# A two-layer block on one core: the first four projection units side by side over quarters of K

## The chip, the core and the metric

The kernel runs on one NeuronCore of a Trainium2 chip. The core has a matrix engine (TensorE, PE in the profile), two elementwise engines (VectorE, DVE, and ScalarE, ACT), GpSimd (POOL) and SyncE (SP), which here only issues DMAs. Each engine works through its own instructions in order. The metric is the device time of one execution in microseconds, the median over several runs.

## What is computed

A first block (normalisation, one wide projection, three kinds of attention over 256 tokens, gated up-projection, output projection, residual) feeds a second one (modulation, two recurrent scans in both directions, a gated feed-forward layer with a convolution). All of it is float32. What matters here is the very first stage:

```python
def rmsnorm(x, g):                       # x: 1 x 256 x 2048
    y = x * lax.rsqrt(jnp.mean(x * x, axis=-1, keepdims=True) + EPS)
    return y * g
hn = rmsnorm(x, norm_g)
proj = jnp.einsum('bsd,dc->bsc', hn, w_in)   # K = d = 2048
br = proj[..., :QKVG_COLS].reshape(b, s, 3, 4, 512)
qa = rmsnorm(to_heads(br[:, :, 0, 0]), ...)  # branch 0: q, then k, v, gate
ka = rmsnorm(to_heads(br[:, :, 0, 1]), ...)
```

## The kernel before

**Precision.** Each float32 operand is split in two parts that TensorE takes at its faster float32 rate: a rounded high part (ScalarE, a copy) and the remainder (VectorE, original less rounded part). A product is then high x high, high x low and low x high. Activations lie as tiles of K, `h(k)` and `l(k)`, 128 x 256 each (K on partitions, tokens along the row), side by side in memory. Weights come in chunks `wr` of 128 x 1024 (eight K tiles of 128 columns), which `Lead.high` rounds into `wh` (ScalarE) and `Lead.low` subtracts into `wl` (VectorE).

**Units.** The projections are a list of units (`f_unit`, L325). A unit makes 128 output columns for all 256 tokens over K = 2048, that is 16 K tiles, as two halves of one chunk each. For every K tile there is one wide matmul (`wh` against `h(k)` and `l(k)` together, 512 columns) and one narrow one (`wl` against `h(k)`, 256 columns); in odd pieces of a unit the narrow ones go first. All accumulate in one accumulator `pm`, of which there are four. After its last half a unit's `post` joins the two column halves (one ScalarE and one VectorE instruction) and gives the accumulator back; in branch 0 the result is later multiplied by the row factor `r1`, since the first projection runs on x times gain, and the normalisation by the mean square is put in afterwards.

**Order.** `first_block` (L850) queues, for branch 0, four units of k, four of q, the forget rows, v and the gate. The program is one loop over `flat`, the list of (unit, half); every engine's order is the order in which this loop writes instructions. For entry i it issues the weight load of entry i + 7, rounds up to i + 4, subtracts up to i + 3, advances side tasks by one step (`W.step`), then issues the matmuls of entry i. There are five `wr` buffers, so the load of chunk e waits until chunk e - 5 has been rounded and subtracted; all weight loads are issued by SP, in order. There are five `wh` and four `wl` buffers.

**The opening.** `start` (L589) runs ahead of the loop. SP loads x's first quarter (`xs[0]`, in two pieces), weight chunk 0, `xs[1]`, chunk 1, `xs[2]` and `xs[3]`; ScalarE's queue loads the first 96 columns of a vector of small parameters (with the gain of the norm at `V_NG`), GpSimd the rest and an identity. Then, quarter by quarter, the 16 x tiles are multiplied by the gain, rounded (ScalarE) and subtracted (VectorE, L200), with chunks 0 and 1 in between. `stats`, a side task, squares the four quarters of x (ScalarE), sums them (three VectorE additions), and sums over partitions by matmuls against ones (`ssq_rstd`, accumulator `ps`), from which `r1` comes; it begins at the loop's second entry, and its matmuls stand in TensorE's order ahead of those of entry 6. `norm1` waits for `r1`, makes the normalised activations for the other branches and starts the modulation work, which streams a large weight through VectorE as filler. A helper records each operation, so many instructions share a line: L166 is every matmul, L184 every ScalarE copy, L191 every two-input VectorE operation.

Of the kernel before, what the change touches and what calls it, by code (L numbers as in the profile page):

```python
# [12 lines left out]
AF = mybir.ActivationFunctionType  # L13
ALU = mybir.AluOpType
# [5 lines left out]
KT = D // 128  # L20
# [109 lines left out]
def trunk_kernel(  # L130
# [50 lines left out]
    def act(out, in_, func, **kw):  # L181
        W.cost["act"] += width(out) / 1200.0 + 0.18
        load_table(func)
        nc.scalar.activation(out=out, in_=in_, func=func, **kw)  # L184
# [105 lines left out]
    def col(c, n=1):  # L290
        return vec[:, c:c + n]
# [30 lines left out]

    units, rush = [], set()

    def f_unit(src, acts, post, nk=KT, k0=0, first=True, last=True, box=None, cols=512, folded=False):  # L325

        box = box if box is not None else {}
        if folded:  # L330
            cols = 256

        def pre():
            box["a"] = acts()
            if first:
                W.take("pm")
                box["acc"] = pm((128, cols))

        def pe(i, h, l):
            acc, a = box["acc"], box["a"]  # L340
            n = min(8, nk - 8 * i)
            end = last and 8 * i + n == nk
            ks = [(k0 + 8 * i + j, slice(j * 128, j * 128 + 128)) for j in range(n)]
            if cols == 512:

                def wide():
                    for k, w in ks:
                        mm(acc, lhsT=h[:, w], rhs=a.both(k), start=k == 0, stop=end and k == k0 + nk - 1)

                def narrow():  # L350
                    for k, w in ks:
                        mm(acc[:, 0:256], lhsT=l[:, w], rhs=a.h(k), start=False, stop=False)

                for part in (narrow, wide) if i % 2 else (wide, narrow):
                    part()
                return
            for k, w in ks:
                stop = end and k == k0 + nk - 1
                if folded:
                    w = slice(w.start, w.start + 96)  # L360
                    if k:
                        mm(acc[0:96, :], lhsT=h[:, w], rhs=a.l(k), start=False, stop=False)
                    mm(acc, lhsT=h[:, w.start:w.start + 128], rhs=a.h(k), start=k == 0, stop=stop)
                    if k == 0:
                        mm(acc[0:96, :], lhsT=h[:, w], rhs=a.l(k), start=False, stop=False)
                else:
                    mm(acc, lhsT=h[:, w], rhs=a.h(k), start=k == 0, stop=False)
                    mm(acc[:, 0:256], lhsT=h[:, w], rhs=a.l(k), start=False, stop=False)
                    mm(acc, lhsT=l[:, w], rhs=a.h(k), start=False, stop=stop)

        halves = [(c * 128, min(8, nk - c) * 128) for c in range(0, nk, 8)]
        units.append(Unit(src, halves, pe, pre, (lambda: W.spawn(post(box["acc"]), urgent=True)) if last else None, folded))
        return box

# [214 lines left out]
    def start():  # L589
        W.room["s4"] -= 4 + 8 + 2  # L590
        xs = [slot() for _ in range(4)]
        u = Acts()
        nc.scalar.dma_start(out=vec[:, 0:V_QK], in_=vec_d[:, 0:V_QK])
        load_table(AF.Ln)
        for i in (0, 2):
            nc.sync.dma_start(out=xs[0][:, i:i + 2, :], in_=xT[:, i:i + 2, :])
        lead.load(0)
        nc.sync.dma_start(out=xs[1], in_=xT[:, 4:8, :])
        lead.load(1)
        nc.sync.dma_start(out=xs[2], in_=xT[:, 8:12, :])  # L600
        nc.sync.dma_start(out=xs[3], in_=xT[:, 12:16, :])
        nc.gpsimd.dma_start(out=vec[:, V_QK:NV], in_=vec_d[:, V_QK:NV])
        nc.gpsimd.dma_start(out=ident, in_=ident_d)
        nc.gpsimd.memset(ones, 1.0)
        nc.gpsimd.memset(epsc, EPS)
        nc.gpsimd.memset(hot, 0.0)
        nc.gpsimd.memset(hot[:, 7:8], 1.0)
        for j in range(4):
            u.more()
            for i in range(4):  # L610
                k = 4 * j + i
                g = col(V_NG + k)
                act(out=u.h(k), in_=xs[j][:, i, :], func=AF.Copy, scale=g)
                stt(out=u.l(k), in0=xs[j][:, i, :], scalar=g, in1=u.h(k), op0=ALU.mult, op1=ALU.subtract)
            if j < 2:
                lead.low(j)
        st["u"] = u

        def stats():
            yield from rest(1)  # L620
            tot = slot()
            for j in range(4):
                q = slot() if j else tot
                act(out=q, in_=xs[j], func=AF.Square)
                yield
                if j:
                    tt(out=tot, in0=tot, in1=q, op=ALU.add)
            yield
            r = yield from ssq_rstd([tot[:, j, :] for j in range(4)])
            give(s4=2)  # L630
            st["r1"] = r
            yield from rest(3)
            yield from grab(ps=1)
            p = ps((128, 2))
            for b in range(2):
                mm(p[:, b:b + 1], lhsT=r[0:1, b * 128:b * 128 + 128], rhs=ones[0:1, 0:1], start=True, stop=True)
            vcopy(rT, p)
            give(ps=1)
            st["rT"] = True

        def norm1():
            yield from until_has("r1")
            r = st["r1"]
            act(out=hot_r, in_=hot, func=AF.Copy)
            act(out=act_c, in_=col(V_C, 32), func=AF.Silu)
            W.idle = st["mod"] = W_mod()
            h = Acts()
            yield
            yield from normed(h, xs, r, col(V_NG, 16))
            st["h"] = h  # L650
            yield from grab(s4=1)
            t = cslot(K_LEV)
            yield from rest(4)
            act(out=lmask, in_=t[:, 0:896].rearrange("p (a b) -> p a b", b=128), func=AF.Copy)
            give(s4=1)

        W.spawn(stats(), urgent=True)
        W.spawn(norm1())
        tt(out=sel[0:36, :], in0=ident[0:36, 0:4], in1=ident[0:36, 32:36], op=ALU.add)
        gq = gqk  # L660
        for j in range(4):
            ts(out=gq[:, j:j + 1], in0=col(V_QK + j), scalar1=SCALE if j % 2 == 0 else 1.0, scalar2=None, op0=ALU.mult)

    gqk = cp.tile([128, 4], F32, name="gqk")
    rT = cp.tile([128, 2], F32, name="rT")
# [184 lines left out]
    def first_block():  # L850
        it = iter(range(10 ** 6))
        nxt = lambda: w1[next(it)]
        for n in range(NB):
            b = {}
            source = u1 if n == 0 else h1
            for key in "kq":
                for hh in range(NH):
                    def post(p, n=n, b=b, key=key, hh=hh):
# [9 lines left out]
                        if hh == NH - 1:  # L868
# [3 lines left out]
                                b["t" + key] = W.spawn(head_norm(x, gqk[:, j:j + 1]))  # L872
                            if key == "q":
                                W.spawn(attend(n, b))
                    f_unit(nxt(), source, post)
            if n == 0:
                f_unit(wf1, u1, forget_rows, folded=True)

# [1145 lines left out]
    ctx_units()  # L2024
    lat_block()
    ffn()
    flat = [(u, i) for u, x in enumerate(units) for i in range(len(x.halves))]

    class Lead:

# [36 lines left out]
    with tc.manual_schedule():  # L2067
        start()
        for i, (u, j) in enumerate(flat):
            lead.load(i + 7)  # L2070
            if u in rush:
                W.step()
# [165 lines left out]
```

## Time and profile before

| | us |
|---|---|
| median of 3 runs | 2126.79 |
| lowest and highest | 2124.09, 2127.64 |
| the profiled execution, by its own clock | 2121.56 |
| its span, first to last instruction | 2119.8 |

The profiled execution is one run of its own; the time outside its span is 1.8 us. In the rows further down, PE is TensorE's matmuls, PEld its weight loads (which overlap with the matmuls), and an engine's name with a q is its DMA issue or sequencer. A DMA's row gives the time of issue; the landing time is given by the views of a line or tile. "x8" behind a row of the order of time is the number of instructions merged in it, and the bracket tells how long the engine was idle before it and what released it. A matmul's duration includes its run through the array, so consecutive ones overlap; their spacing is shorter than their duration.

### The profile page before, as it was taken

To read this page: it belongs to the slowest core of one execution; us is meant where nothing else is said; L and a number is where in the kernel's file an instruction comes from. 1 tells how busy PE (TensorE), PEld (TensorE's weight loads), DVE (VectorE), ACT (ScalarE), POOL (GpSimd) and SP (SyncE) were. 2 spreads that over 40 slices of the span, in tenths; PEclk is the share of its full clock that TensorE was granted. 3 is DMA by queue.
4 is the path that set the end of the run, shared out by engine and by line. 5 is a ranking of instruction groups with operands and counts; after the bars stand their busy time and mean duration, and the time that the engine had idled before them with its cause. 6 is when DMAs were issued, how large, how long until landed. Compare 5 with 4: busy or idle time off the path is not lost.

```text
span 2119.8 us, 31753 instructions
## 1 busy us (share of the span) xinstructions
PE 2083.6 (98%) x11834; PEld 1814.0 (86%) x11834; DVE 1734.4 (82%) x2499; ACT 1134.5 (54%) x1653; POOL 125.5 (6%) x251
## 2 busy tenths in 40 slices
PE   8999999999999999999999999999999999999997
PEld 6888888998988887888888788888888888888886
DVE  6999897999999988778876757789888888897554
ACT  6765555454545656555645545555555555543542
POOL 0010100000111010110000000000000000021000
PEclk9999999999999999999999999999999999999999
DMA  7686776777799796885444445646555555598653
GB/s 276 230 284 215 260 246 210 257 241 275 271 329 396 251 338 222 312 326 200 162 161 158 149 148 202 223 141 204 194 189 189 189 190 189 187 384 318 197 188 115
DMA packets 140283, 488.52 MB, mean 230 GB/s; under 512 B 15424, under 2 KB 21584, under 8 KB 140128
## 3 DMA queue, kind: packets, MB, share of 16 engines
q1 hardware_dynamic: 105344, 366.13, 48.7%
q0 software_dynamic: 32784, 119.40, 16.2%
q8 instruction: 92, 1.51, 0.3%
q10 hardware_dynamic: 2000, 0.97, 0.2%
q14 instruction: 63, 0.52, 0.1%
HBM read 479.10 MB, written 7.34 MB: 229 GB/s over the span
## 4 chain that ended last, share of the span: by engine, by line
PE 94%; DVE 2%; DMA 1%; issue 1%; ACT 1%; POOL 0%; DVEq 0%; SPq 0%; ACTq 0%; POOLq 0%
PE pm L166 86%; PE ps L166 7%; DMA s<-in_wmod_dram 1%; DVE wl L191 1%; DVE a L200 1%; DVE s L191 1%; ACT wh L184 0%; ACT s L184 0%; DVE s L200 0%; DMA wr<-in_w_dram 0%; PE ps L170 0%; ACT b L184 0%; DVE a L191 0%; ACT L177 0%; DVE b L191 0%
## 5 line engine op out<-in xcount | busy, mean ns | idle before, releaser
L166 PE MATMUL pm<-s,wh 128*128 128x512 f32 (+3 forms) x5019 | 1163.5, 377 | 8.7 <-ACT wh L184 8.7
L184 ACT ACTIVATE wh<-wr 128x1024 fp32r<-128x1024 f32 x706 | 727.8, 1034 | 627.5 <-PE pm L166 488.8
L166 PEld LDWEIGHTS pm<-s,wh 128*128 128x128 f32 (+1 forms) x5019 | 898.0, 189 | 164.3 <-ACT wh L184 8.7
L191 DVE TENSOR_TENSOR wl<-wr,wh 128x1024 fp32r<-128x1024 f32 (+2 forms) x700 | 826.2, 1192 | 186.3 <-issue 82.6
L166 PE MATMUL pm<-s,wl 128*128 128x256 f32 (+1 forms) x4635 | 657.9, 283 | 9.2 <-DVE wl L191 7.4
L166 PEld LDWEIGHTS pm<-s,wl 128*128 128x128 f32 x4635 | 615.9, 191 | 35.0 <-DVE wl L191 9.0
L200 DVE SCALAR_TENSOR_TENSOR s<-s,act_c,s 128x1024 f32<-128x1024 f32 x240 | 301.8, 1278 | 14.3 <-DMA s<-in_wmod_dram 13.7
L166 PE MATMUL pm<-wh,s 128*128 128x512 f32 x832 | 262.6, 397 | 0.0
L166 PEld LDWEIGHTS pm<-wh,s 128*128 128x128 f32 x832 | 154.3, 188 | 35.4 <-issue 3.3
L166 PE MATMUL pm<-wl,s 128*128 128x512 f32 x416 | 162.3, 390 | 0.0
L200 DVE SCALAR_TENSOR_TENSOR a<-b,vec,a 128x192 f32<-128x192 f32 (+1 forms) x344 | 149.2, 434 | 9.1
L414 POOL DMA_DIRECT2D s<-in_wmod_dram x188 | 99.1, 528 | 931.1 <-DVE s L200 438.0
L191 DVE TENSOR_TENSOR s<-pm,s 128x256 f32<-128x256 f32 x142 | 59.7, 421 | 46.7 <-ACT s L184 45.2
L184 ACT ACTIVATE s<-s 128x256 fp32r<-128x256 f32 (+4 forms) x76 | 62.3, 826 | 66.2 <-DVE s L191 60.6
L166 PEld LDWEIGHTS pm<-wl,s 128*128 128x128 f32 x416 | 78.1, 188 | 16.8
L184 ACT ACTIVATE b<-b 128x512 f32<-128x512 f32 (+3 forms) x88 | 52.3, 600 | 27.1 <-DVE b L191 23.9
L184 ACT ACTIVATE s<-a 128x256 fp32r<-128x256 f32 (+1 forms) x73 | 29.8, 416 | 60.8 <-DVE a L191 46.5
L166 PE MATMUL ps<-s,s 128*128 128x256 f32 (+4 forms) x240 | 59.3, 381 | 0.0
L191 DVE TENSOR_TENSOR s<-s,s 128x1024 fp32r<-128x1024 f32 (+4 forms) x53 | 47.2, 897 | 8.8 <-ACT s L184 8.7
L166 PEld LDWEIGHTS ps<-s,s 128*128 128x128 f32 (+1 forms) x240 | 42.1, 189 | 9.3 <-issue 3.5
L184 ACT ACTIVATE a<-s 128x256 f32<-128x256 f32 x47 | 19.5, 418 | 45.8 <-DVE s L200 31.8
L184 ACT ACTIVATE s<-pm 128x256 f32<-128x256 f32 (+2 forms) x102 | 41.3, 416 | 2.7 <-DVE s L200 2.7
(177 smaller groups left out, 959.9 us busy)
## 6 DMA issues: line engine op xcount, KB each, us to landing
wr<-in_w_dram SPq DMA_DIRECT2D x192, 512.0 KB, 4.7
s<-in_wmod_dram POOLq DMA_DIRECT2D x188, 512.0 KB, 7.0
wr<-in_wup_dram SPq DMA_DIRECT2D x188, 512.0 KB, 4.0
wr<-in_wlat_dram SPq DMA_DIRECT2D x96, 512.0 KB, 3.7
wr<-in_wdown_dram SPq DMA_DIRECT2D x80, 512.0 KB, 4.6
wr<-in_wout_dram SPq DMA_DIRECT2D x64, 512.0 KB, 4.6
wr<-in_wctx_dram SPq DMA_DIRECT2D x48, 512.0 KB, 4.9
s<-in_cst_dram POOLq DMA_DIRECT2D x9, 512.0 KB, 5.6
```

Source lines behind the costliest of these rows:

```text
L166: nc.tensor.matmul(out, lhsT=lhsT, rhs=rhs, start=start, stop=stop)
L184: nc.scalar.activation(out=out, in_=in_, func=func, **kw)
L191: nc.vector.tensor_tensor(out=out, in0=in0, in1=in1, op=op)
L200: nc.vector.scalar_tensor_tensor(out=out, in0=in0, scalar=scalar, in1=in1, op0=op0, op1=op1)
L414: (nc.sync if i < 4 else nc.gpsimd).dma_start(out=tiles[i], in_=wmod[k, :, ch, :])
```

## The change

The four units of k in branch 0 run side by side: all four on the first quarter of K, then all four on the second, and so on, each with its own accumulator. Their weights come in chunks of 128 x 512 (four K tiles), 16 of them, so `flat` has eight entries more. `start` loads and works only x's first quarter and chunks 0 to 3, with `xs[1]` issued behind chunk 3. The other twelve x tiles are made one per entry of the loop, by a task that is advanced first in each entry; it also issues the loads of `xs[2]` (entry 4) and `xs[3]` (entry 8) on SP. The second piece of `xs[0]` goes to ScalarE's queue, and so do the 16 gain columns alone; the rest of the vector goes to GpSimd in two pieces. The statistics begin eight steps later, and the selector and gain preparation moves into them.

```diff
--- before.py
+++ after.py
@@ -322,7 +322,7 @@
 
     units, rush = [], set()
 
-    def f_unit(src, acts, post, nk=KT, k0=0, first=True, last=True, box=None, cols=512, folded=False):
+    def f_unit(src, acts, post, nk=KT, k0=0, first=True, last=True, box=None, cols=512, folded=False, step=8):
 
 
 
@@ -338,9 +338,9 @@
 
         def pe(i, h, l):
             acc, a = box["acc"], box["a"]
-            n = min(8, nk - 8 * i)
-            end = last and 8 * i + n == nk
-            ks = [(k0 + 8 * i + j, slice(j * 128, j * 128 + 128)) for j in range(n)]
+            n = min(step, nk - step * i)
+            end = last and step * i + n == nk
+            ks = [(k0 + step * i + j, slice(j * 128, j * 128 + 128)) for j in range(n)]
             if cols == 512:
 
                 def wide():
@@ -368,7 +368,7 @@
                     mm(acc[:, 0:256], lhsT=h[:, w], rhs=a.l(k), start=False, stop=False)
                     mm(acc, lhsT=l[:, w], rhs=a.h(k), start=False, stop=stop)
 
-        halves = [(c * 128, min(8, nk - c) * 128) for c in range(0, nk, 8)]
+        halves = [(c * 128, min(step, nk - c) * 128) for c in range(0, nk, step)]
         units.append(Unit(src, halves, pe, pre, (lambda: W.spawn(post(box["acc"]), urgent=True)) if last else None, folded))
         return box
 
@@ -590,34 +590,50 @@
         W.room["s4"] -= 4 + 8 + 2
         xs = [slot() for _ in range(4)]
         u = Acts()
-        nc.scalar.dma_start(out=vec[:, 0:V_QK], in_=vec_d[:, 0:V_QK])
+        nc.scalar.dma_start(out=vec[:, V_NG:V_NG + 16], in_=vec_d[:, V_NG:V_NG + 16])
+        nc.scalar.dma_start(out=xs[0][:, 2:4, :], in_=xT[:, 2:4, :])
         load_table(AF.Ln)
-        for i in (0, 2):
-            nc.sync.dma_start(out=xs[0][:, i:i + 2, :], in_=xT[:, i:i + 2, :])
-        lead.load(0)
+        nc.sync.dma_start(out=xs[0][:, 0:2, :], in_=xT[:, 0:2, :])
+        lead.load(3)
         nc.sync.dma_start(out=xs[1], in_=xT[:, 4:8, :])
-        lead.load(1)
-        nc.sync.dma_start(out=xs[2], in_=xT[:, 8:12, :])
-        nc.sync.dma_start(out=xs[3], in_=xT[:, 12:16, :])
-        nc.gpsimd.dma_start(out=vec[:, V_QK:NV], in_=vec_d[:, V_QK:NV])
+        for c in (slice(0, V_NG), slice(V_NG + 16, NV)):
+            nc.gpsimd.dma_start(out=vec[:, c], in_=vec_d[:, c])
         nc.gpsimd.dma_start(out=ident, in_=ident_d)
         nc.gpsimd.memset(ones, 1.0)
         nc.gpsimd.memset(epsc, EPS)
         nc.gpsimd.memset(hot, 0.0)
         nc.gpsimd.memset(hot[:, 7:8], 1.0)
-        for j in range(4):
-            u.more()
-            for i in range(4):
-                k = 4 * j + i
-                g = col(V_NG + k)
-                act(out=u.h(k), in_=xs[j][:, i, :], func=AF.Copy, scale=g)
-                stt(out=u.l(k), in0=xs[j][:, i, :], scalar=g, in1=u.h(k), op0=ALU.mult, op1=ALU.subtract)
-            if j < 2:
-                lead.low(j)
+
+        def first_tile(k):
+
+            if k % 4 == 0:
+                u.more()
+            g = col(V_NG + k)
+            act(out=u.h(k), in_=xs[k // 4][:, k % 4, :], func=AF.Copy, scale=g)
+            stt(out=u.l(k), in0=xs[k // 4][:, k % 4, :], scalar=g, in1=u.h(k), op0=ALU.mult, op1=ALU.subtract)
+
+        for k in range(4):
+            first_tile(k)
+            if k % 2:
+                lead.high(k // 2)
+        lead.low(1)
+
+        def more_tiles():
+            for k in range(4, KT):
+                if k % 4 == 0 and k > 4:
+                    nc.sync.dma_start(out=xs[k // 4], in_=xT[:, k:k + 4, :])
+                first_tile(k)
+                yield
+
+        st["more_tiles"] = Task(more_tiles())
         st["u"] = u
 
         def stats():
-            yield from rest(1)
+            yield from rest(9)
+            tt(out=sel[0:36, :], in0=ident[0:36, 0:4], in1=ident[0:36, 32:36], op=ALU.add)
+            gq = gqk
+            for j in range(4):
+                ts(out=gq[:, j:j + 1], in0=col(V_QK + j), scalar1=SCALE if j % 2 == 0 else 1.0, scalar2=None, op0=ALU.mult)
             tot = slot()
             for j in range(4):
                 q = slot() if j else tot
@@ -656,10 +672,6 @@
 
         W.spawn(stats(), urgent=True)
         W.spawn(norm1())
-        tt(out=sel[0:36, :], in0=ident[0:36, 0:4], in1=ident[0:36, 32:36], op=ALU.add)
-        gq = gqk
-        for j in range(4):
-            ts(out=gq[:, j:j + 1], in0=col(V_QK + j), scalar1=SCALE if j % 2 == 0 else 1.0, scalar2=None, op0=ALU.mult)
 
     gqk = cp.tile([128, 4], F32, name="gqk")
     rT = cp.tile([128, 2], F32, name="rT")
@@ -872,7 +884,7 @@
                                 b["t" + key] = W.spawn(head_norm(x, gqk[:, j:j + 1]))
                             if key == "q":
                                 W.spawn(attend(n, b))
-                    f_unit(nxt(), source, post)
+                    f_unit(nxt(), source, post, step=4 if (n, key) == (0, "k") else 8)
             if n == 0:
                 f_unit(wf1, u1, forget_rows, folded=True)
 
@@ -2024,7 +2036,9 @@
     ctx_units()
     lat_block()
     ffn()
-    flat = [(u, i) for u, x in enumerate(units) for i in range(len(x.halves))]
+
+    flat = [(u, i) for i in range(4) for u in range(4)]
+    flat += [(u, i) for u, x in enumerate(units) if u > 3 for i in range(len(x.halves))]
 
     class Lead:
 
@@ -2067,6 +2081,7 @@
     with tc.manual_schedule():
         start()
         for i, (u, j) in enumerate(flat):
+            st["more_tiles"].advance()
             lead.load(i + 7)
             if u in rush:
                 W.step()
```

## Rows read from the trace of the kernel before

**Rows 1.** The page: busy time of the engines, and shares of the chain.

```profile
PE 2083.6 (98%) x11834; PEld 1814.0 (86%) x11834; DVE 1734.4 (82%) x2499; ACT 1134.5 (54%) x1653; POOL 125.5 (6%) x251
...
PE 94%; DVE 2%; DMA 1%; issue 1%; ACT 1%; POOL 0%; DVEq 0%; SPq 0%; ACTq 0%; POOLq 0%
```

**Rows 2.** Busy time by stretches of 53 us, columns in the first row.

```profile
core 0: us, PE busy (x) PEld busy (x) DVE busy (x) ACT busy (x) POOL busy (x), PEclk, DMA share, GB/s
0.00:53.00 53.00, 42.55 (x230) 36.30 (x231) 35.80 (x58) 34.44 (x51) 1.82 (x10) 1.00 0.75 276
53.00:106.00 53.00, 53.00 (x281) 45.78 (x280) 48.02 (x80) 40.07 (x64) 3.48 (x7) 1.00 0.66 230
...
1378.00:1431.00 53.00, 48.48 (x358) 45.65 (x357) 45.71 (x85) 31.00 (x59) 0.00 (x0) 1.00 0.40 140
```

**Rows 3.** Chain that ended last, opening: start us, us, what.

```profile
1.66 5.95 DMA wr<-in_w_dram
...
28.41 1.15 DVE s L191
```

**Rows 4.** TensorE's order of time, opening: start us, us, instructions [idle, releaser].

```profile
8.74 3.53 PE L166 MATMUL pm<-s,wh 128*128 128x512 f32 x8 [8.74 <-ACT wh L184]
...
14.89 3.80 PE L166 MATMUL pm<-s,wh 128*128 128x512 f32 x16
18.53 2.08 PE L166 MATMUL pm<-s,wl 128*128 128x256 f32 x16
...
29.69 1.97 PE L166 MATMUL ps<-s,ones 128*128 128x256 f32 x8 [1.67 <-DVE s L191]
...
35.25 3.82 PE L166 MATMUL pm<-s,wh 128*128 128x512 f32 x16
```

**Rows 5.** SP's issues, landings of L598, chunk 1, L600; SP's waits to 45.

```profile
2.12 0.43 SPq L598 DMA_DIRECT2D s<-in_xT_dram  x1
2.60 0.80 SPq L2044 DMA_DIRECT2D wr<-in_w_dram  x1
3.44 0.43 SPq L600 DMA_DIRECT2D s<-in_xT_dram  x1
3.92 0.46 SPq L601 DMA_DIRECT2D s<-in_xT_dram  x1
...
DMA to landing us min/median/max: 6.6/6.6/6.6
...
DMA to landing us min/median/max: 7.4/7.4/7.4
...
DMA to landing us min/median/max: 7.8/7.8/7.8
...
SPq L2044 <- DVE wl L191: 29.6, 14, 4.7
```

**Rows 6.** Weight loads of 512 KB, issued 17 to 21 and 35 to 42.

```profile
DMA to landing us min/median/max: 3.4/5.4/5.6
...
DMA to landing us min/median/max: 3.1/3.1/3.6
```

**Rows 7.** ScalarE's order of time, opening.

```profile
4.39 1.70 ACT L184 ACTIVATE s<-s,vec 128x256 fp32r<-128x256 f32 x4 [1.93 <-DMA vec<-in_vec_dram]
...
11.32 3.29 ACT L184 ACTIVATE s<-s,vec 128x256 fp32r<-128x256 f32 x8
...
14.52 2.97 ACT L184 ACTIVATE wh<-wr 128x1024 fp32r<-128x1024 f32 x3
```

**Rows 8.** VectorE's order of time, opening; then groups by form, whole span.

```profile
12.59 3.25 DVE L200 SCALAR_TENSOR_TENSOR s<-s,vec,s 128x256 fp32r<-128x256 f32 x8
...
16.08 4.62 DVE L191 TENSOR_TENSOR wl<-wr,wh 128x1024 fp32r<-128x1024 f32 x4
...
L191 DVE TENSOR_TENSOR wl<-wr,wh 128x512 fp32r<-128x512 f32 x16 | 10.9, 683 | 0.0
L184 ACT ACTIVATE s<-s 128x512 fp32r<-128x512 f32 x8 | 4.6, 623 | 3.4 <-DVE s L191 3.4
```

## The prediction

> **What bounds the kernel now.** I read the page first, then the stretches, then the chain, then each engine's order of time in the opening. TensorE is busy 98% of the span and carries 94% of the chain that ended last [rows 1]. The stretches show where the missing 2% lies [rows 2]: in the first 53 us it is busy 42.55 (10.45 idle), from 53 to 106 all of 53.00, and of the stretches behind, up to the tail, the one at 1378 lacks most (4.52). From 53 us on, an opening that ends later or earlier moves everything behind it by as much, so the case is decided before the fifth unit.
>
> The chain of the opening runs over the first weight load (1.66, 5.95 us), later over VectorE's last sum of squares (28.41) [rows 3]. TensorE's order of time says it in full [rows 4]: nothing until 8.74, eight wide matmuls in 3.53 (0.44 each, against 16 in 3.80 a little later), one gap of 1.67 ahead of the eight sum-of-squares matmuls at 29.69 (released by VectorE), and the row at 35.25 holds the last eight wide matmuls of the fourth unit and the first eight of the fifth. So the fifth unit (index 4) begins at 35.25 + 8 x 0.229 = **37.1**; that is the mark I compare with (0.229 is the spacing: 16 in 3.80, less one's 0.39 duration, over 15 starts). Narrow ones follow at (2.08 - 0.28)/15 = 0.12. A chunk of four K tiles costs TensorE 4 x (0.229 + 0.12) = 1.39, a unit 5.6.
>
> **The change part by part.**
>
> *Smaller first chunk, fewer loads ahead of it.* The first weight load halves to 256 KB and the second half of x's first quarter goes to ScalarE's queue. The first load landed at 1.66 + 5.95 = 7.6 behind 512 KB of x; with about half the bytes ahead it lands after 4.4, when the first x tile is rounded [rows 7], and before 7.6; I take 6. ScalarE's rounding takes 0.6 [rows 8]; TensorE starts near 6.6, 2.1 earlier. This is all that the edit can win at the front.
>
> *Same matmuls, other order.* Sixteen chunks of half size replace eight: the same 64 wide and 64 narrow matmuls, the same weight loads. Eight more rounding and eight more subtracting instructions at half the size cost only the fixed part of each: ScalarE's 128x256 comes every (3.29 - 0.50)/7 = 0.40, its 128x1024 every 0.96 [rows 7], so 128x512 about 0.585, twice that 0.2 over one large: 8 x 0.2 = 1.7 us on ScalarE. VectorE likewise: 0.395 and 1.13, so 0.60 for 128x512 (one lasts 0.68) [rows 8], 8 x 0.07 = 0.6 us. Eight DMA issues of 0.4 on SP's queue hide, since SP mostly waits [rows 5].
>
> *x's third and fourth quarter behind the weights.* This decides. Before, all of x is issued by 4.4 [rows 5], ahead of every load that waits for a buffer. Afterwards quarter 2 is issued by SP in iteration 4, behind the load of chunk 10, and quarter 3 in iteration 8, behind that of chunk 14. There are five weight buffers, so chunk 10's load waits until VectorE has subtracted chunk 5, and chunk 14's until it has subtracted chunk 9; the waits of SP on exactly this are there before (29.6 us, 14 times) [rows 5], but no x stands behind them. The wait spreads: on ScalarE, tile 8's rounding waits for quarter 2 and everything later is queued behind it; on VectorE tile 8's subtraction stands ahead of chunk 7's, for which TensorE and SP's chunk 12 wait. So I follow the chain (h = rounding of an x tile, H of a weight chunk, l and L the subtractions):
> 1. Quarter 1 is issued behind four chunks: 2 MB in all have passed when it lands. Before, the load that completes 2 MB is the second weight load: 2.60 + 7.4 = 10.0. Bounds: the 1.5 MB load, 2.12 + 6.6 = 8.7, and the 2.5 MB load, 3.44 + 7.8 = 11.2 [rows 5]. I take **10.0**.
> 2. ScalarE then does h4, H2, H3, H4, h5, H5 (2 x 0.40 + 4 x 0.585 = 3.14), then h6 (0.50); VectorE l6 (0.40) and L5 (0.70): 4.74. SP issues chunk 10, then quarter 2 (0.45): quarter 2 is issued at **+5.2**.
> 3. It lands after λ. Loads of 512 KB in a quiet queue took 3.1 to 3.6, four issued 1.1 us apart 3.4 to 5.6 [rows 6]. Two chunks of 256 KB stand right ahead of ours; nearer to the first of these than to the last, I take **λ = 3.9** and keep 3.1 and 5.6 as ends.
> 4. h8, H8, h9, H9 (1.97), h10 (0.50), l10, L9 (1.10), chunk 14's issue (0.45): quarter 3 is issued **+4.05** after quarter 2 landed, and takes λ again.
> 5. Then ScalarE has four x tiles, four chunks and, since the statistics now begin at iteration 9, the squares of x between them: h12, H12, h13, H13, square, h14, H14, square: h15 begins 4.87 after the landing. VectorE goes on from it: 0.50 + l15 0.40 + L14 0.60 + sum 1.13 + L15 0.60 + sum 1.13 + L16 (full size) 1.13 + last sum 1.22 = 6.7. The last sum ends **+11.6** after quarter 3 landed, and the sum-of-squares matmuls, in program order ahead of chunk 14's, wait for it. By then TensorE has been idle: h15 also gates chunk 12, so chunks 12 and 13 end at +5.4 + 0.2 + 0.5 (l15 and the last wide) + 1.7 = +7.8, a gap of 3.8.
> 6. Sum-of-squares matmuls 1.6, chunks 14 and 15 2.8: the fifth unit begins **+4.4** later.
>
> Sum: 10.0 + 5.2 + 4.05 + 11.6 + 4.4 + 2λ = 35.25 + 2λ = **43.05**, against 37.1: **+6.0 us**. With λ = 3.1 it is +4.4, with 5.6 +9.4; quarter 1 at its ends moves that by -1.3 or +1.2. The earlier start of TensorE lies wholly beside this chain.
>
> The Trainium skill ("DMA: Bandwidth & Descriptors", Anatomy of one DMA) fits a transfer as 2.0 us plus bytes over 436 GB/s. By that estimate λ is 3.2 and the sum +4.6; the quiet rows agree with it (3.1 at the least), those with others ahead do not, and I go by the rows.
>
> *Small edits.* The column of gains is loaded by itself on ScalarE's queue and the rest of the vector by GpSimd; before, the first rounding waited for the vector until 4.39 [rows 7], so a few tenths either way, off the chain. The selector and gain instructions move to iteration 9, 0.3 us on VectorE ahead of h14's work: covered while VectorE waits for h14 and h15, 0.3 if not. The fifth unit needs the first unit's accumulator: its join stands right behind the last sum, ends 0.3 + 0.1 after it while the sum-of-squares matmuls run, nothing. Behind the opening no edit is made; the holes behind, as that at 1378, may move by 1 us each way, as the planner counts steps and there are eight more.
>
> **The rivals.**
> *A. Quarters 2 and 3 arrive in time* (SP is not held, or issues them earlier than program order says). Against it: SP's loads go out in order, each right behind a subtraction. Then ScalarE runs from quarter 1 without a break: 11 h (4.4), 13 H (7.6), two squares (1.9) put h15 at 23.9, or 1.6 later where chunk 5 lands late behind 1 MB of x; +6.7 +4.4 gives 35.0 to 36.6, so -2.1 to -0.5: no change that can be told.
> *B. TensorE is fed from 6.6 on:* 22.3 of matmuls, 1.6 for the sum of squares and 1.5 for the slow first eight end at 32.0, **-5.1**. It needs λ so small that x is never waited for, and the statistics not behind it; TensorE's four chunks of a quarter take 5.6, the loop of steps 3 and 4 at least 3.1 + 4.05 = 7.2, so it can't keep up: it decides where λ is under 1.5, half of the least row.
> *C. TensorE slows after its long idle.* After 8.7 idle its first eight wide matmuls took twice their later time, after 1.67 idle the next ones did not [rows 4], though the granted clock reads 1.00 in every stretch [rows 2]. The 3.8 gap of step 5 lies between. If it counts, up to 4.4 of work runs at half pace until it recovers: +2 to +3 on the forecast, +8 to +9. The Trainium skill ("TensorE: Matmul & The Clock Gate", the HAM clock gate) has the array fall to half its clock when idle and recover with sustained work; this gap's length no row settles.
>
> **How the numbers follow.** Forecast 0.64, A 0.18, B 0.07, C 0.11. The profiled execution took 2121.56 (span 2119.8 and 1.8 around it), under the lowest of the three runs (2124.09): it becomes 2127.6, and the median 2126.79 becomes **2132.8**. The bound of 0.2%, about what a measurement of this kernel can tell from no change, is 4.25 us. Of the forecast, about 0.08 lies under +4.25 (quick λ and an early quarter 1), so slower 0.56 + 0.11 = 0.67, same 0.18 + 0.08 = 0.26, faster 0.07 (B; it is the only case over 4.25). Range: B and A's lower half left out below (-2.3), the upper end from λ = 5.6 with a late quarter 1 (+10.7): 2124.5 to 2137.5.
>
> **What would show it.** Right: quarter 2 issued near 15, quarter 3 near 23, each right behind a weight load that waited for VectorE; ScalarE idle 2 to 4 us ahead of h8 and h12, released by x; TensorE idle about 4 ahead of the sum-of-squares matmuls, which begin near 38 to 39; the fifth unit near 43. The first matmul near 6.6 shows the front right. Wrong: x's quarters landed before 17 and 24, or TensorE without holes from 12 on; or a hole behind, as that at 1378, that is smaller by as much, which would mean the opening is not paid in full.

## The result

| | before | after |
|---|---|---|
| median of 4 runs each, us | 2126.35 | 2141.72 |
| lowest to highest, us | 2124.09 to 2127.64 | 2138.07 to 2145.72 |
| profiled execution (its span), us | 2121.56 (2119.8) | 2141.92 (2140.1) |

Before has one run more here than in its table above, hence the other median. The ratio is 1.0074, 95% interval 1.0054 to 1.0094: the change costs 15.4 us. The forecast was 2132.8 in a range of 2124.5 to 2137.5: the direction was right, the size was not, and the time lies over the range.

The stretches of after, as in [rows 2] (columns: us, busy time with instructions of TensorE, its weight loads, VectorE, ScalarE, GpSimd; then the clock granted to TensorE as a share of 2.4 GHz, the DMA engines' busy share, GB/s):

```profile
0.00:53.00 53.00, 38.33 (x164) 31.59 (x165) 28.99 (x55) 28.77 (x50) 2.35 (x11) 0.87 0.61 206
53.00:106.00 53.00, 53.00 (x282) 45.60 (x281) 43.26 (x74) 35.01 (x56) 2.42 (x5) 1.00 0.73 251
106.00:159.00 53.00, 49.75 (x284) 43.16 (x283) 51.27 (x70) 34.26 (x52) 4.72 (x9) 1.00 0.72 261
```

Two things differ. In the first 53 us TensorE is idle for 14.7 instead of 10.45, and its clock reads 0.87 where it read 1.00 before. And the stretch at 106 has a hole of 3.25 us; before, TensorE is busy there for all of 53.00.

TensorE's order of time in after, opening (start us, us, instructions, idle time ahead and its releaser), which answers to [rows 4]:

```profile
6.62 2.14 PE L166 MATMUL pm<-s,wh 128*128 128x512 f32 x4 [6.62 <-ACT wh L184]
...
18.25 1.09 PE L166 MATMUL pm<-s,wh 128*128 128x512 f32 x4
23.38 1.22 PE L166 MATMUL pm<-s,wl 128*128 128x256 f32 x4 [4.04 <-DVE wl L191]
24.40 3.62 PE L166 MATMUL pm<-s,wh 128*128 128x512 f32 x8
...
35.83 0.58 PE L166 MATMUL pm<-s,wl 128*128 128x256 f32 x1 [1.48 <-ACT s L184]
...
42.19 3.42 PE L166 MATMUL ps<-s,ones 128*128 128x256 f32 x8 [2.17 <-DVE s L191]
...
47.52 2.89 PE L166 MATMUL pm<-s,wh 128*128 128x512 f32 x12
```

The first matmul is 2.1 us earlier, as forecast, and the gain is spent by 23.38. The sum of squares takes 3.42 instead of 1.97 us. The fifth unit begins behind four of the last row's twelve: 47.52 + 4 x 0.229 = **48.4**, against 37.1 before and 43.05 in the forecast.

x's quarters 2 and 3: the issues with their time to landing, then ScalarE's first rounding behind quarters 1, 2 and 3, then VectorE's last sum of squares.

```profile
L624 SPq DMA_DIRECT2D s<-in_xT_dram x2: 423/424/424, 15.9 to 25.8; - x2
...
  ACT s L184: 10.7, 2
...
DMA to landing us min/median/max: 4.8/5.3/5.8
```

```profile
10.88 0.51 ACT L184 ACTIVATE s<-s,vec 128x256 fp32r<-128x256 f32 x1 [3.00 <-DMA s<-in_xT_dram]
...
21.70 0.51 ACT L184 ACTIVATE s<-s,vec 128x256 fp32r<-128x256 f32 x1 [5.54 <-DMA s<-in_xT_dram]
...
30.61 0.51 ACT L184 ACTIVATE s<-s,vec 128x256 fp32r<-128x256 f32 x1 [5.13 <-DMA s<-in_xT_dram]
```

```profile
40.83 1.21 DVE L191 TENSOR_TENSOR s<-s,s 128x1024 f32<-128x1024 f32 x1
```

ScalarE stands still for 5.54 and 5.13 us for quarters 2 and 3: the chain of the forecast is there, with longer links. The clock by stretches of after shows what came on top: it falls in the idle time from 19.34 on, and the stretches behind run at 0.73 to 0.81 on average, which is 2.4 GHz for part of them and 1.2 for the rest.

```profile
19.34:23.38 4.04, 0.00 (x1) 0.00 (x0) 1.14 (x3) 1.68 (x4) 0.00 (x0) 0.84 0.31 112
23.38:33.40 10.02, 9.77 (x41) 8.30 (x41) 5.18 (x14) 4.89 (x10) 0.00 (x0) 0.73 0.49 163
33.40:42.19 8.79, 5.02 (x16) 3.73 (x17) 7.62 (x13) 7.90 (x12) 0.00 (x0) 0.81 0.84 291
42.19:48.40 6.21, 6.21 (x24) 5.24 (x25) 2.76 (x5) 2.63 (x6) 0.00 (x0) 0.73 0.51 175
```

Set against the same matmuls of before, after is late by 11.3 us at the fifth unit, by 9 to 11 until 142, by 16.3 at 174, 19.0 at 380 and 20.4 at the end. (The profiled execution of before, 2121.56, lies under all four of its runs; by the medians 15.4 are lost, not 20.4.) The step between 142 and 174 is a hole with no counterpart before. TensorE's and ScalarE's order of time there, after:

```profile
157.13 1.57 PE L166 MATMUL ps<-b,s 128*128 128x256 f32 x8 [3.25 <-ACT b L184]
```

```profile
154.70 1.06 ACT L184 ACTIVATE s<-s 128x1024 f32<-128x1024 f32 x1 [4.63 <-DVE s L191]
155.66 1.04 ACT L184 ACTIVATE wh<-wr 128x1024 fp32r<-128x1024 f32 x1
156.61 0.85 ACT L184 ACTIVATE b<-ps 128x384 f32<-128x384 f32 x2
```

The attention's matmuls wait for a copy (b) by ScalarE, which is queued behind a piece of side work (s, the modulation) that ScalarE holds for VectorE for 4.63 us. Before, that piece stands elsewhere in the queue.

### The profile page after: what moved, and what is told of

It reads as the page before. It is cut to its first block, busy times and chain, and to the rows that moved or that the text cites. A ratio compares the mean times of both kernels' runs of the same rounds, so it can differ in the third digit from the quotient of the medians.

```text
span 2140.1 us, 31808 instructions
## 1 busy us (share of the span) xinstructions
PE 2096.5 (98%) x11834; PEld 1823.4 (85%) x11834; DVE 1735.5 (81%) x2507; ACT 1135.2 (53%) x1661; POOL 126.1 (6%) x252
## 4 chain that ended last, share of the span: by engine, by line
PE 92%; DVE 3%; DMA 2%; ACT 1%; issue 1%; POOL 0%; SPq 0%; DVEq 0%; ACTq 0%; POOLq 0%
PE pm L166 85%; PE ps L166 7%; DMA s<-in_wmod_dram 1%; DVE wl L191 1%; DMA s<-in_xT_dram 1%; ACT s L184 1%; DVE s L191 1%; DVE a L200 0%; DVE s L200 0%; ACT wh L184 0%; PE ps L170 0%; DMA wr<-in_w_dram 0%; ACT b L184 0%; ACT L177 0%; SPq L2058 0%
## 5 line engine op out<-in xcount | busy, mean ns | idle before, releaser
L184 ACT ACTIVATE wh<-wr 128x1024 fp32r<-128x1024 f32 (+1 forms) x714 | 729.2, 1025 | 631.9 <-PE pm L166 484.4
L191 DVE TENSOR_TENSOR wl<-wr,wh 128x1024 fp32r<-128x1024 f32 (+1 forms) x708 | 827.6, 1180 | 185.5 <-PE pm L166 84.8
L166 PE MATMUL pm<-s,wl 128*128 128x256 f32 (+1 forms) x4635 | 664.1, 285 | 15.1 <-DVE wl L191 11.7
L191 DVE TENSOR_TENSOR s<-s,s 128x1024 fp32r<-128x1024 f32 (+4 forms) x53 | 47.2, 897 | 8.8 <-ACT s L184 8.7
```

The lines of the kernel that those rows point to most:

```text
L166: nc.tensor.matmul(out, lhsT=lhsT, rhs=rhs, start=start, stop=stop)
L191: nc.vector.tensor_tensor(out=out, in0=in0, in1=in1, op=op)
```

## The experiments

Theory: the loss is the opening, where x stands behind the weights, and beside it the planner's order behind the opening. Its backlog at the end of the fourth unit is 4.86 (VectorE) and 4.04 (ScalarE) where it was 3.74 and 2.60, since eight more instructions on each engine are charged a fixed part (0.14 us each on VectorE, 0.18 on ScalarE, in the program's own cost table), and it places side work by that backlog. Rivals: the clock is the larger part; the queue on which x is issued; the place of the statistics. All against runs of before on the same chip; the fifth unit's start is read in each trace as above (37.1 before, 48.4 after). The ratio is the recorded one with its interval, not the quotient of the two medians (e3_both: 1.0017, the medians alone give 1.0022); 0.001 is 2.1 us. In e9 and e10 four small matmuls (0.5 us) that stand behind the fifth unit's start elsewhere stand ahead of it.

| run | ratio [95%] | median less before's, us | fifth unit at | idle ahead of the sum of squares |
|---|---|---|---|---|
| e1_order | 1.0062 [1.0038, 1.0086] | +11.7 | 49.8 | 2.1 |
| e2_xearly | 1.0042 [1.0029, 1.0056] | +7.6 | 38.8 | 3.0 |
| e3_both | 1.0017 [1.0002, 1.0033] | +4.6 | 38.9 | 3.2 |
| e4_before_order | 1.0024 [1.0014, 1.0034] | +4.2 | 37.6 | 1.5 |
| e5_filler | 1.0054 [1.0040, 1.0067] | +11.3 | 48.6 | filled |
| e6_own_queue | 1.0056 [1.0043, 1.0070] | +12.3 | 47.2 | 3.7 |
| e7_best | 1.0039 [1.0026, 1.0053] | +9.1 | 43.1 | 6.3 |
| e8_stats_later | 1.0070 [1.0056, 1.0084] | +15.4 | 51.6 | 6.8 |
| e9_stats_early | 1.0034 [1.0022, 1.0045] | +8.3 | 44.1 | 3.7 |
| e10_late_x_early_stats | 1.0061 [1.0045, 1.0076] | +13.0 | 49.7 | 4.4 |
| e11_sum_behind | 0.9994 [0.9985, 1.0003] | -1.8 | 35.3 | none |

### Opening and planner apart

e1_order keeps the change and gives the planner the old backlog, so that side work behind the opening is ordered as before; e4_before_order is the kernel before with the new backlog.

```diff
 # e1_order: after, end of the loop over chunks
+            if i == 15:
+                W.back = dict(dve=3.74385, act=2.5976)
 # e4_before_order: before, same place
+            if i == 7:
+                W.back = dict(dve=4.86385, act=4.0376)
```

> The changed kernel, but at the end of entry 15 the planner's backlog is set to the numbers that the kernel before has at the same place (VectorE 3.74 and ScalarE 2.60 where the change has 4.86 and 4.04). From the fifth unit on every engine's order is then that of the kernel before; the opening is the changed one. Theory 1 (two losses: 11.3 us in the opening, from x's quarters behind the weights, and some 5 us near 150 from side work in another order): the fifth unit begins at 48.4 as in the changed kernel, the hole of 5 us between 142 and 160 is gone, about 5 us under the changed kernel, +10 on the kernel before. Rival (the hole near 150 follows from the late opening, since the modulation's loads then come late): no change against the changed kernel, +15.

> The kernel before, with the planner's backlog at the end of its fourth unit set to what the changed kernel has there (VectorE 4.86, ScalarE 4.04), so that from the fifth unit on all engines have the changed kernel's order; the opening is untouched. Theory 1: the hole near 150 appears alone, +5 us. Rival (it needs the late opening): within 1 us of the kernel before.

Alone, the opening costs 11.7 and the order 4.2; together 15.9, and the whole change 15.4. The intervals are wide (8 to 18 us for e1_order, 3 to 7 for e4_before_order, 11 to 20 for the change), so that the two add up is shown to a few us only. The fifth unit of e1_order was expected at 48.4 and came at 49.8: its two landings of x took 6.2 and 5.8 us. From the fifth unit on e1_order has before's order of instructions on TensorE, VectorE and ScalarE, and e4_before_order has after's. In e1_order TensorE has no wait between 136 and 168; its interval alone would not rule out the rival's +15, this trace and e4_before_order do. In e4_before_order the opening is untouched and the hole appears 11 us earlier, with the same queue ahead of it; the same matmuls are 1.0 us earlier than in before at 140 and 3.6 later at 174 (TensorE, then ScalarE):

```profile
145.94 1.57 PE L166 MATMUL ps<-b,s 128*128 128x256 f32 x8 [2.92 <-ACT b L184]
```

```profile
143.51 1.06 ACT L184 ACTIVATE s<-s 128x1024 f32<-128x1024 f32 x1 [4.64 <-DVE s L191]
144.47 1.04 ACT L184 ACTIVATE wh<-wr 128x1024 fp32r<-128x1024 f32 x1
145.42 0.85 ACT L184 ACTIVATE b<-ps 128x384 f32<-128x384 f32 x2
```

So some 4 us of the loss come from a number in the program's own planner, 100 us behind the edit.

### x early

e2_xearly issues quarters 2 and 3 right behind the load of chunk 4, ahead of the loads of the loop; e3_both adds e1_order's two lines.

```diff
         nc.sync.dma_start(out=xs[1], in_=xT[:, 4:8, :])
+        lead.load(4)
+        nc.sync.dma_start(out=xs[2], in_=xT[:, 8:12, :])
+        nc.sync.dma_start(out=xs[3], in_=xT[:, 12:16, :])
...
-                if k % 4 == 0 and k > 4:
-                    nc.sync.dma_start(out=xs[k // 4], in_=xT[:, k:k + 4, :])
```

> The changed kernel with x's quarters 2 and 3 issued in the opening, behind quarter 1 and chunk 4, so that no x load stands behind a weight load that waits. Everything else stays, the side work's order too. Theory 1: ScalarE no longer waits 5 us twice for x; the fifth unit begins at 37 to 39 (by the same sums, with ScalarE running through) instead of 48.4, so about 10 us under the changed kernel, +4 to +7 on the kernel before, what is left being the side work's order. Rival (half-size weight chunks and their loads cost the time, wherever x stands): the fifth unit stays beyond 45 and the time within 4 us of the changed kernel.

> Both edits: x's quarters issued early and the planner's backlog of the kernel before at entry 15. Theory 1 (the two losses add): -1 to +3 us on the kernel before. Rival for the first edit: +9 or more; rival for the second: as the kernel with x early alone.

With x early ScalarE waits for neither quarter, and the opening shrinks from +11.3 to +1.7 (38.8, as expected). The times missed: e2_xearly is +7.6 where +4 to +7 was expected, e3_both +4.6 where -1 to +3 was; by the medians x early saves 7 to 8 us, not 10. The rival of e2_xearly falls by the opening. In e3_both the hole near 150 (3.23 us in e2_xearly) is gone, though the intervals of the two kernels overlap. What is left of the opening is one gap. e2_xearly, TensorE's order of time, then the stretches over that gap:

```profile
30.11 1.09 PE L166 MATMUL pm<-s,wh 128*128 128x512 f32 x4
34.22 1.97 PE L166 MATMUL ps<-s,ones 128*128 128x256 f32 x8 [3.01 <-DVE s L191]
35.83 0.82 PE L166 MATMUL pm<-s,wl 128*128 128x256 f32 x4
...
37.88 2.91 PE L166 MATMUL pm<-s,wh 128*128 128x512 f32 x12
```

```profile
31.20:34.20 3.00, 0.00 (x1) 0.01 (x1) 3.00 (x4) 2.19 (x4) 0.00 (x0) 1.00 0.85 300
34.20:44.20 10.00, 9.98 (x56) 8.80 (x56) 7.87 (x15) 5.08 (x9) 0.00 (x0) 1.00 0.52 163
```

Chunks 14 and 15 could run in it but stand behind the sum in TensorE's program. e3_both is 2.7 slower than its opening shows (4.6 against 1.9); its trace is late by 3.0 from 110 to 340, behind which the granted clock falls in two later holes (360 and 1292) that both kernels have and that the profiled execution of before passes at full clock.

### The clock's part

```diff
+            for e, n in ((7, 16), (12, 12), (14, 13)):
+                if i == e:
+                    warm = ps()
+                    for k in range(n):
+                        nc.tensor.matmul(warm, lhsT=st["u"].h(1)[:, 0:128], rhs=st["u"].both(0), start=True, stop=True)
```

> The changed kernel with 41 matmuls more that nothing reads (128x512, as wide as the unit's own): 16 ahead of the eighth chunk, 12 ahead of the thirteenth and 13 ahead of the sum of squares, where TensorE would be idle; the planner is not told of them. It asks what the half clock costs of the 11.3 us by which the fifth unit is late. Theory (x behind the weights and its long landings are the loss; most half-pace work lies beside the wait for x): no granted clock under 1 in the opening, sum of squares in 2.0 instead of 3.4 us, the fifth unit near 46.6 instead of 48.4, whole time 1 to 2.5 us under the changed kernel, about +13 against before. Rival (the clock is the larger part): the fifth unit near 43 and +9 or less against before.

The filler keeps the clock at 1.00 up to 33.4; a gap of 2.79 that it didn't cover then brought one fall. e5_filler, TensorE's order of time and stretches:

```profile
20.00 3.80 PE L2094 MATMUL ps<-s 128*128 128x512 f32 x16
...
33.42 1.22 PE L166 MATMUL pm<-s,wl 128*128 128x256 f32 x4 [2.79 <-DVE wl L191]
...
44.07 1.89 PE L166 MATMUL ps<-s,ones 128*128 128x256 f32 x8
```

```profile
23.64:33.40 9.76, 6.93 (x37) 5.39 (x36) 3.95 (x9) 3.66 (x9) 0.00 (x0) 1.00 0.49 163
33.40:44.07 10.67, 10.65 (x46) 9.01 (x47) 9.50 (x18) 9.03 (x13) 0.00 (x0) 0.84 0.81 260
```

The fifth unit is no earlier (48.6), but x's quarter 3 landed 1.13 later here (31.72 against 30.59), and the last sum ends 11.44 behind it, in after 11.45: up to there the half clock costs nothing, as ScalarE, VectorE and x set the pace (in after no wait of ScalarE or VectorE ends on TensorE before 45). Behind it, after takes 6.4 us to the fifth unit and e5_filler 4.5 from the first of these matmuls. The clock's part of the opening is thus under 2 us. The rival falls; the predicted 46.6 was missed too, for the later landing (1.1) and a filler that, its middle part partly at half clock, ended 0.9 behind the last sum. By the medians e5_filler is 11.3 behind before and after 15.4, though its opening is no shorter; the two intervals overlap, and the traces show about 2 us of this difference, most of it later falls of the clock. The rest is not explained.

### The queue

```diff
-                    nc.sync.dma_start(out=xs[k // 4], in_=xT[:, k:k + 4, :])
+                    nc.scalar.dma_start(out=xs[k // 4], in_=xT[:, k:k + 4, :])
```

> The changed kernel with x's quarters 2 and 3 issued at the same places of the program, but by ScalarE on its own queue, where no weight load stands ahead. Theory (a landing takes 5.8 and 4.8 us because two weight loads stand right ahead on the queue): landings of 3.5 to 4 after the issue, the fifth unit 2 to 3 us earlier than 48.4, the time 2 to 3 us under the changed kernel (+12 to +13 against before). Rival (the engines that move the data are shared, the queue makes no difference): landings again 5 to 6, no change against the changed kernel (+15).

```profile
L624 ACTq DMA_DIRECT2D s<-in_xT_dram x2: 334/334/334, 16.5 to 23.0; - x2
...
DMA to landing us min/median/max: 3.8/4.8/5.9
```

Neither theory holds for both. Quarter 2, issued while three weight loads of the other queue were under way, again took 5.9; quarter 3, issued 5.8 us after the last weight load, when none was under way, took 3.8. In after three were under way at either issue (5.77 and 4.83). These landings go with what is under way, not with the queue; no run varies that alone. Quarter 3 went out 2.7 earlier, since ScalarE's queue does not wait for buffers, and landed 3.7 earlier; only 1.2 reached the fifth unit: from the landing to the last sum it took 1.2 longer than in after, because chunks then were late (ScalarE waited 1.1 for one), and from there on 1.3 longer, because more of it ran at half clock (the sum of squares 3.75 us behind 3.65 idle; granted clock 0.54 against 0.73). The median, +12.3, lies in the first theory's window without its gain in the opening: that is luck, or the spread of the medians.

### The place of the statistics

Four kernels move them. e7_best and e9_stats_early have x early, e8_stats_later and e10_late_x_early_stats have it where the change puts it. In e7_best and e9_stats_early quarter 2 is issued behind chunk 4 and quarter 3 in the loop's second entry. All four set the backlog at the place of e1_order (VectorE 3.0 and ScalarE 1.5, in e9 and e10 4.4 and 2.3), to keep before's order behind the opening: e7 and e8 have it from about 60 us on, e9 and e10 from about 115. The diff shows only the place of the statistics.

```diff
 # e7_best, e8_stats_later:                   rest(11)
 # e9_stats_early, e10_late_x_early_stats:    rest(5)
-            yield from rest(9)
+            yield from rest(11)
```

> The changed kernel with quarter 2 of x issued right behind chunk 4 in the lead-in and quarter 3 in the second iteration, the statistics started two steps later, so that the sum of squares stands behind chunk 15 and not ahead of chunk 14, and the planner's backlog set behind the fourth unit so that side work behind the opening comes in the order of the kernel before. Theory: no wait for x or for chunk 5, none of 3 us for the sums, so the fifth unit begins near 34.6 against 37.1 before, no hole near 150, and the time is 2.5 us under before (ratio near 0.9988). Rival: VectorE's last sum still ends near 34 to 35 and the sum of squares waits for it, the fifth unit near 36 to 37: within 1 us of before.

> The changed kernel, x where the change puts it, with the statistics started two steps later (sum of squares behind chunk 15) and the order of side work behind the opening as in the kernel before (as in e1_order, its counterpart). Theory: the sums of squares stand ahead of chunks 14 and 15 for 2 us and more, which come off, so the fifth unit begins 3.5 to 4.5 us earlier than in e1_order, near 46, and the time is near +8 against before. Rival (x's last quarter is all that is late): the fifth unit near 49 to 50 and +11 to +12 as in e1_order.

> The kernel of e7_best with the statistics started six steps earlier: the squares of x stand at iterations 5 to 8, while TensorE still has chunks to do, and the sum of squares near iteration 10; the planner's backlog is set so that side work behind the opening comes nearly in the order of the kernel before. Theory (in e7_best, e8_stats_later and the changed kernel the sums stand behind roundings that wait for TensorE's buffers or for x): TensorE never waits long for a sum, the fifth unit begins near 35 against 37.1 before, no half clock in the opening, and the time is 2 us under before (ratio near 0.999). Rival (VectorE becomes the bound, with four sums of 1.1 between the subtractions of x): tile 15's subtraction comes 2 to 3 us later than in e2_xearly, the fifth unit near 37 to 38, and the time equals before within 2 us.

> The changed kernel, x's quarters where the change puts them, with the squares of x at iterations 5 to 8 and the same setting of the planner's backlog as e9_stats_early. It is the counterpart of e1_order and e8_stats_later. Theory (the last sum of squares is the last link of the opening): three of the four squares are done while x's last quarter is under way, so the last sum ends near 35 and the sum of squares waits no more behind chunk 13; the fifth unit begins near 43 to 44 (e1_order 50.3, e8_stats_later 51.6) and the time is +5 to +7 against before. Rival (x's last quarter alone is late): the fifth unit near 47 or later and +10 against before.

All four theories fell; of the rivals only e10_late_x_early_stats's came near (47 or later, +10 at the least). TensorE's sum of squares in e7_best, e8_stats_later, e9_stats_early and e10_late_x_early_stats:

```profile
39.91 3.75 PE L166 MATMUL ps<-s,ones 128*128 128x256 f32 x8 [6.31 <-DVE s L191]
```

```profile
48.41 3.58 PE L166 MATMUL ps<-s,ones 128*128 128x256 f32 x8 [6.76 <-DVE s L191]
```

```profile
30.46 3.75 PE L166 MATMUL ps<-s,ones 128*128 128x256 f32 x8 [3.71 <-DVE s L191]
```

```profile
35.97 3.75 PE L166 MATMUL ps<-s,ones 128*128 128x256 f32 x8 [4.39 <-DVE s L191]
```

Later, the sums stand on VectorE between the fifth unit's large subtractions (1.22 each) and the joins; earlier, they stand between the subtractions of x's last tiles, and TensorE reaches the eight matmuls before VectorE reaches the last sum. Either way the gap grows, and behind each of these gaps the matmuls run at 1.2 GHz (the granted clock reads 0.50 over each of the four). In e7_best the fifth unit comes 4.2 us later than in e3_both.

### The sum behind chunk 15

What remained was to leave the squares and the sums where they are and move only the eight matmuls. In the diff the setting of the backlog (dve=3.0, act=1.5 at i == 15) is left out.

```diff
         nc.sync.dma_start(out=xs[1], in_=xT[:, 4:8, :])
+        lead.load(4)
+        nc.sync.dma_start(out=xs[2], in_=xT[:, 8:12, :])
...
-                if k % 4 == 0 and k > 4:
-                    nc.sync.dma_start(out=xs[k // 4], in_=xT[:, k:k + 4, :])
+                if k == 4:
+                    lead.load(5)
+                    nc.sync.dma_start(out=xs[3], in_=xT[:, 12:16, :])
...
-            yield
+            yield from rest(3)
             r = yield from ssq_rstd([tot[:, j, :] for j in range(4)])
```

> The changed kernel with x early (quarter 2 right behind chunk 4, quarter 3 right behind chunk 5), the squares of x and their sums where the change has them, but the sum-of-squares matmuls three steps later in TensorE's program, behind chunk 15; the planner's backlog is set so that side work behind the opening comes in the order of the kernel before. It differs from e7_best in that the squares and the sums are not moved, from e2_xearly in the place of the eight matmuls. Theory (what was wrong with e7_best and e8_stats_later is that the sums themselves moved behind roundings that wait for TensorE; what is late in e2_xearly is only that chunks 14 and 15 stand behind the sum): the gap of 3.0 before the sum of squares goes, TensorE does chunks 14 and 15 in it, the fifth unit begins near 35 to 36 against 37.1 before, no half clock in the opening, and the time is 1 to 2 us under before (ratio 0.999 to 0.9995). Rival (any later place of the sum of squares holds the fifth unit's own roundings and the joins): the fifth unit at 38 or later, the time within 0.1% above e3_both's ratio of 1.0017.

```profile
32.54 1.09 PE L166 MATMUL pm<-s,wh 128*128 128x512 f32 x4
33.67 1.97 PE L166 MATMUL ps<-s,ones 128*128 128x256 f32 x8
35.29 2.21 PE L166 MATMUL pm<-s,wh 128*128 128x512 f32 x8
```

The gap is gone and the fifth unit begins at 35.3, 1.8 earlier than before. The median is 2122.62 (11 runs) against 2124.44 (15 runs): 1.8 under, as expected, with an interval that still holds no change at all. It beats the changed kernel by far (0.9994 against 1.0074) and can't be told from the kernel before.

## Why the prediction was wrong in size

The chain of steps 1 to 6, link by link:

| link | forecast | measured |
|---|---|---|
| 1. quarter 1 lands | 10.0 | 10.85 |
| 2. to the issue of quarter 2 | 5.2 | 5.06 |
| 3. its landing (λ) | 3.9 | 5.77 |
| 4. to the issue of quarter 3 | 4.05 | 4.08 |
| its landing (λ) | 3.9 | 4.83 |
| 5. to the end of the last sum | 11.6 | 11.45 |
| 6. to the fifth unit | 4.4 | 6.40 |
| sum | 43.05 | 48.44 |

(Link 4's own terms add up to 4.02.)

- **The front** was right: first matmul at 6.62 (6.6).
- **The chain** was right, and the links of instructions up to the last sum (2, 4, 5) to 0.15 us. SP is held as forecast, ScalarE and VectorE go through the tiles in the order worked out, and the last sum sets the end. That x is what binds is shown by e2_xearly: without the two waits 9.6 of the opening's 11.3 go.
- **λ** was mis-sized: 3.9 was taken as nearer to the quiet rows, and the rows said 3.4 to 5.6 for a load with others ahead [rows 6]. "Two chunks right ahead" was short too: three were under way at each issue. 5.77 lies even above that end; the two landings carry 2.8 of the 5.4 us that the opening missed by. The Trainium skill's fit ("DMA: Bandwidth & Descriptors", Anatomy of one DMA), which gave 3.2, is further off; the page gives it for transfers issued by GpSimd, and x's are issued by SP. Of the landings of quarters 2 and 3 in after and e6_own_queue only the one with no weight load under way at its issue comes near it (3.8).
- **Quarter 1** cost another 0.85, within its stated bounds.
- **Step 6 with rival C.** The rival was given a chance of 0.11 and came on top of the forecast, not in its place: the granted clock fell to half, first in the 4.04 us of idle ahead of 23.38, a wait for quarter 2 that C did not look at. Its price was put at 2 to 3 us behind a gap of 3.8 ahead of the sum; the link took 2.0 longer than its 4.4, nearly all of it the clock (e2_xearly needs 4.6 for the same matmuls at 1.00), behind smaller gaps (1.48 and 2.17) in a stretch that had idled before. The gap ahead of the sum was 2.17 and not 3.8, because chunks 12 and 13, partly at half clock, ended 1.6 later than forecast, at no cost. C's remark that the clock reads 1.00 over the slow first matmuls shows nothing: the traces hold no clock record of the first 11.8 us, and a stretch without one reads 1.00; in after, too, the first four wide matmuls take 2.14 where four later take 1.09. The Trainium skill ("TensorE: Matmul & The Clock Gate", the HAM clock gate) has the array fall to half when idle; this trace agrees (0.84 in the idle stretch from 19.34, 0.73 behind it, where before read 1.00).
- **The holes behind** "may move by 1 us each way": this is the step that failed outright, a term put at nothing. The eight more instructions were costed at their time on the engines (2.3 us, off the path), but not at what the planner's backlog makes of them. That moved side work from 50 to 210 us, and made a hole near 150: 4.2 us by e4_before_order (interval 3 to 7). Steps were named as what the planner counts; it also counts charged cost.
- **Rivals A and B** did not come. A's sign, that x in time costs nothing, is borne out only by e11_sum_behind, where also the eight matmuls had to move.

Together: 5.4 in the opening and about 4 for the order make 9.4 more than the forecast's 6.0, which is the 15.4 measured. That it comes out so exactly is luck, given the intervals; the two traces differ by 11.3, 5.0 and, for later falls of the clock, 4.1.

One thing stays open. In the traces later holes (near 360, 1290, 1415 and 1950) pass with or without a fall of the clock; each fall near 360 or 1290 costs 1.4 to 2.7 us. After has these two, and the profiled execution of before none. Why a given execution falls there was not settled; it is probably part of the spread of the medians, and of e3_both's 2.7 us.

## What to carry to other kernels

When a load that the next link needs is put behind loads that wait for buffers, each trip round (issue, landing, work, free buffer) is a serial link: price the landing with what is under way at that time, at the upper end of the rows, not with a quiet one. Where a planner orders work by charged cost, an edit that adds instructions in one place can move side work far behind it; compare the order of the queues behind the edit before costing it at nothing. Of a reduction that several engines share, try moving the consumer behind the independent work with the producers left where they are: here that closed the gap (e11_sum_behind), and four kernels that moved the producers widened it.

## What the hardware showed that was not expected

- The length of the last idle stretch alone does not say whether the clock falls. Behind 3.01 us (e2_xearly at 34.2) and 2.92 us (e4_before_order at 145.94) the granted clock stays at 1.00; behind 2.79 us (e5_filler at 33.4) it reads 0.84 for the next 10.67 us, and the sum of squares takes 3.75 us behind 3.65 to 6.31 us of idle.
- A load of 512 KB took 5.77 and 4.83 us with three weight loads of 256 KB under way on the same queue at its issue (after), 5.9 with three on another and 3.8 with none (e6_own_queue).
- The kernel before alone ran from 2119.59 to 2129.41 us in 19 runs on one chip, with a mean granted clock of 0.998 in the fastest and 0.993 to 0.994 in the two slowest. The spread is half a per cent of the time, and the slower runs mostly have the lower clock, not strictly (2120.97 and 2126.66 both at 0.996).
